# A third row buffer for the first stage's convolutions, in the room of the gates' small tiles

## The chip, the cores and the metric

The kernel runs on one core of one Trainium2 chip. The metric is the device time of one execution in microseconds (us). The core has engines that run side by side and wait for each other by semaphores: PE (TensorE: matmuls and transposes, with its weight loads, PEld), DVE (VectorE), ACT (ScalarE), POOL (GpSimd) and SP (SyncE, which here only issues DMAs). Each engine takes its instructions in the order in which the program gives them. SBUF is the working memory, 128 partitions; sizes below are in bytes of one partition.

## The reference

One layer of an encoder over 16 meta tokens and 1024 tokens of width 1024. What the change touches is in branch A, a gated DeltaNet with 8 heads:

```
h = rmsnorm(h_res, norm1_w[l])
proj = h @ w_in[l]
(q, k, v, z, b_raw, a_raw, sc_b, sc_c, sc_x, gate_a, gate_b) = jnp.split(proj, SPLIT_POINTS, axis=-1)
o_dn = gated_deltanet_bidir(q, k, v, z, b_raw, a_raw, ...)
y_b = (sc_b * depthwise_conv_centred(sc_c * sc_x, sc_conv_w[l])) @ w_branch_sc[l]
...
# in gated_deltanet_bidir
qkv = jax.nn.silu(depthwise_conv_centred(jnp.concatenate([q, k, v], axis=-1), conv_w))
beta = jax.nn.sigmoid(b_raw)
g = -jnp.exp(A_log) * jax.nn.softplus(a_raw + dt_bias)
o_fwd = chunk_gated_delta_rule(qp, kp, vp, gp[:, :, 0], bp[:, :, 0])
o_bwd = flip(chunk_gated_delta_rule(flip(qp), flip(kp), flip(vp), flip(gp[:, :, 1]), flip(bp[:, :, 1])))
```

Each of q, k and v goes through a centred convolution of five taps and SiLU; branch B has a convolution of three taps (the "short" one). beta and g, the gates, are small: 16 columns of b and 16 of a for each token. The scan of a head goes over chunks, forward and backward at once. What follows (merge, output projection, SwiGLU, last norm) is in later stages that the change leaves alone.

## The kernel before, in words

Every matmul in fp32 accuracy is made of three passes over operands split into a high and a low part, so PE does most of the work. The first stage (to about 1000 us) computes the input projection column block by column block, and the DeltaNet scans between.

**Units of dense work.** A unit is one block of 128 columns of `w_in`. `pick` (L922) gives out the next: K, Q, V of each head (`u_qkv`, L366; the order is in `qkv_units`, L906), then fill units: z (`u_z`), the short convolution's C, X and B (`u_short`, L416), and gates (`u_gate`). Which kind comes is set by how far the scans have got (`qkv_ok`). The matmuls of a unit are at L331.

**Rows.** A K, Q or V unit writes its result, 1040 columns wide in three chunks, twice by ACT: plain into a *row* (L387), and times the middle tap into `kq` or `vT` (L388). The row is a tile `ra` of 1044 floats, 4,176 bytes, from `row_buffer` (L339); POOL clears its edges (L385, L386). A short unit C also takes a row (its edge is cleared at L424), and X multiplies into the same row (L428, L431).

**Jobs.** The convolution of a row is vector work that is spread over time. `conv_job` (L347) makes it in two halves; in each, four operations at L354 add the outer taps, ACT takes the tanh (L359) and one operation at L362 finishes SiLU. The `yield` behind each tells the time at which the next step may be written. `short_job` (L401) is the same for the short convolution (L405, L410), `fs_job` (L483) is the elimination of a head's triangular systems: 62 small vector operations in turn (L490, L494).

**The planner.** The order of all instructions in this stage is written out when the program is made. Four clocks `T` estimate where each engine is. After each three matmuls, `run_streams` (L966) advances the heads' streams that are due: `g_decay`, `g_norm` (L530), `g_inv` (L622, which starts `fs_job`) and `g_scan` (L744); then `pump` (L302) writes out steps of jobs until DVE's clock is 700 ns past PE's. Jobs stand in lanes (conv, short, fs, norm); of the lanes that are ready the one with the least weighted time spent is served (`WEIGHT`, L267: 1.0 for conv and short, 0.33 for fs). Only the first job of a lane runs.

**Forcing.** A new row needs a free buffer. `row_buffer` therefore calls `force` (L258) on the job of the last row but one: it writes out all that is left of that job, and of jobs before it in its lane, at once, whatever the steps' ready times. The list `raws` holds the jobs in the order of their rows.

**Streams of a head.** `g_norm` starts when the K and Q jobs of its head are done. It turns k and q (copies from L560 on), makes norms (cc, L592), and later products of k and q (L582, with L612 and L616 on DVE). `g_inv` sends blocks through DRAM, starts the elimination, sends back, and finishes with small matmuls (L705 to L736). `g_scan` turns v into `vS` (L763), and for each step makes r on DVE (L805), which PE needs at L813; its output leaves at L898. A product loop starts when the decay factors of its head are there, and those wait for the scan before the last.

**The gates.** `g_gates` (L1200) runs once, early in the stage, between dense work: ACT and DVE make beta and the decays in tiles BA, a_, e_, z_, z2, sr and two gc, from the pool c1, 4,608 bytes together; PE reads gc at L1267 and L1279. They are not used again. `vS`, the scans' turned values, is a single buffer of 9 x 128 floats, 4,608 bytes, in the pool dn.

Of the kernel before, what the change touches and what calls it, by code (L numbers as in the profile page):

```python
# [8 lines left out]
F32 = mybir.dt.float32  # L9
# [7 lines left out]
P = 128  # L17
# [20 lines left out]
def encoder_layer(ctx: ExitStack, tc: tile.TileContext, x, meta, norm1_w, w_in,  # L38
# [16 lines left out]
    def uid(s):  # L55
        cnt["n"] += 1
        return f"{s}_{cnt['n']}"
# [144 lines left out]
    c1 = ph1.enter_context(tc.tile_pool(name="c1", bufs=1))  # L202
    d1 = ph1.enter_context(tc.tile_pool(name="d1", bufs=1))
# [14 lines left out]
    def on(e, ns, ready=0.0):  # L218

        T[e] = max(T[e], ready, T["pe"]) + ns  # L220
        return T[e] + TOPE
# [8 lines left out]
    def A(n):  # L230
        return on("act", 144 + 0.834 * n)
# [26 lines left out]
    def force(job):  # L258

        for q in lanes.values():  # L260
            if job in q:
                while not job.done:
                    while not q[0].done:
                        q[0].step()
                    q.pop(0)
# [71 lines left out]
    raws = []  # L337

    def row_buffer():  # L339
        if len(raws) >= 2:  # L340
            force(raws[-2])
        return d1.tile([P, 1044], F32, tag="ra", name=uid("ra"), bufs=2)

    def half_buffer():
        return d1.tile([P, 520], F32, tag="rb", name=uid("rb"), bufs=3)
# [20 lines left out]
    def u_qkv(h, i, w):  # L366
# [12 lines left out]
        for ci, (t0, n) in enumerate(QUERY if i == 1 else QCH):  # L379
            po = psm()  # L380
            yield from dense_steps(po, w, hx, t0, n, sweep=(h == i == ci == 0))
            if raw is None:
                raw = row_buffer()
                if i != 1:
                    nc.gpsimd.memset(raw[:, 0:2], 0.0)  # L385
                nc.gpsimd.memset(raw[:, L + 2:L + 4], 0.0)  # L386
            nc.scalar.copy(raw[:, 2 + t0:2 + t0 + n], po[:, :n])  # L387
            nc.scalar.activation(dst[:, t0:t0 + n], po[:, :n], AF.Copy, scale=wc[:, 2, col:col + 1])  # L388
            A(n)
            A(n)  # L390
            sub["rows"] = 2 + t0 + n if ci < 2 else L + 4
            if ci == 1:
                job = enqueue("conv", conv_job(raw, dst, col, sub, META if i == 1 else 0))
                raws.append(job)
# [21 lines left out]
    def u_short(j, i, w):  # L416
        st_ = shorts[j]
        if i < 2:
            for t0, n in ((14, 322), (336, 320), (656, 384)):
                po = psm()  # L420
                yield from dense_steps(po, w, hx, t0, n)
                if "cx" not in st_:
                    st_["cx"] = row_buffer()
                    nc.gpsimd.memset(st_["cx"][:, 1026:1028], 0.0)  # L424
                    raws.append(Job(iter(())))
                sl = st_["cx"][:, t0 - 14:t0 - 14 + n]
                if i == 0:
                    nc.scalar.copy(sl, po[:, :n])  # L428
                    A(n)
                else:  # L430
                    nc.vector.tensor_tensor(out=sl, in0=po[:, :n], in1=sl, op=ALU.mult)  # L431
                    V(n)
            if i == 1:
                st_["yc"] = []
                st_["job"] = enqueue("short", short_job(st_["cx"], j, st_["yc"]))
                raws[st_["ri"]] = st_["job"]
            else:
                st_["ri"] = len(raws) - 1
        else:
            for i2 in range(2):  # L440
                po = psm()
                yield from dense_steps(po, w, hx, META + 512 * i2, 512)
                force(st_["job"])
                yc = st_["yc"][i2][:, :512]
                nc.vector.tensor_tensor(out=yc, in0=po, in1=yc, op=ALU.mult)
                V(512)
                nc.sync.dma_start(p_d[j][:, 512 * i2:512 * i2 + 512], yc)
# [752 lines left out]
    def g_gates():  # L1200

        small_v = lambda: on("dve", 240)
        BA = c1.tile([P, 9, 32], F32, name="BA")
        dtb, alg = (c1.tile([P, 16], F32, name=n) for n in ("dtb", "alg"))
        nc.sync.dma_start(dtb, dt_bias.rearrange("a b c -> a (b c)").broadcast_to([P, 16]))
        nc.sync.dma_start(alg, A_log.rearrange("a b c -> a (b c)").broadcast_to([P, 16]))
        nc.gpsimd.memset(BA, 0.0)
        gcs = [c1.tile([P, 8, 9], F32, name=f"gc{d}") for d in range(2)]
        for gc in gcs:
            nc.gpsimd.memset(gc, 0.0)  # L1210
        pba = psd()
# [1 line left out]
        for c in range(9):  # L1213
            t0, p = (META + c * P, P) if c < 8 else (0, META)
# [3 lines left out]
        pv = pba.rearrange("p (c a n) -> p c a n", c=8, a=2)  # L1218
        nc.scalar.copy(BA[:, 0:8], pv[:, :, 0])
        nc.scalar.copy(BA[:META, 8], pbm[:META, 0:32])  # L1220
        A(512)
        yield T["act"] + HOP
        nc.vector.tensor_tensor(out=BA[:, 0:8], in0=pv[:, :, 1], in1=BA[:, 0:8], op=ALU.add)
        nc.vector.tensor_tensor(out=BA[:META, 8], in0=pbm[:META, 32:64], in1=BA[:META, 8], op=ALU.add)
        a_ = c1.tile([P, 9, 16], F32, name="a_")
        nc.vector.tensor_tensor(out=a_, in0=BA[:, :, 16:32], in1=dtb.unsqueeze(1).broadcast_to([P, 9, 16]), op=ALU.add)
        e_ = c1.tile([P, 9, 16], F32, name="e_")
        nc.vector.tensor_scalar(out=e_, in0=a_, scalar1=-1.0, scalar2=None, op0=ALU.mult)
        nc.vector.tensor_tensor(out=e_, in0=e_, in1=a_, op=ALU.min)
        yield on("dve", 1400)  # L1230
# [2 lines left out]
        nc.scalar.activation(beta, BA[:, :, 0:16], AF.Tanh, scale=0.5)  # L1233
        A(400)
        yield T["act"] + HOP
        z_ = c1.tile([P, 9, 16], F32, name="z_")
        nc.vector.tensor_scalar(out=z_, in0=e_, scalar1=2.0, scalar2=None, op0=ALU.add)
        nc.vector.reciprocal(z_, z_)
        nc.vector.tensor_tensor(out=z_, in0=z_, in1=e_, op=ALU.mult)
        z2 = c1.tile([P, 9, 16], F32, name="z2")  # L1240
        nc.vector.tensor_tensor(out=z2, in0=z_, in1=z_, op=ALU.mult)
        on("dve", 900)
        yield T["dve"]
        sr = c1.tile([P, 9, 16], F32, name="sr")
        nc.vector.tensor_scalar(out=sr, in0=z2, scalar1=2.0 / 17, scalar2=2.0 / 15, op0=ALU.mult, op1=ALU.add)
        small_v()
        for k in (13, 11, 9, 7, 5, 3, 1):
# [51 lines left out]
    dn = ph1.enter_context(tc.tile_pool(name="dn", bufs=1))  # L1299
    meta_inv = [dn.tile([P, P], F32, name=f"meta_inv{i}") for i in range(2)]  # L1300
    for m_ in meta_inv:
        nc.gpsimd.memset(m_, 0.0)
    SPL = (4, 6, 8, 10)
    decs.append([g_gates(), T["pe"], None])
    while done < H or qkv_units or fill_units or any(ahead):
        u = ahead.pop(0)
# [595 lines left out]
```

## Time and profile before

| | |
|---|---|
| median of three runs | 1979.19 us (1978.93 to 1982.11) |
| the profiled execution | 1981.91 us |
| its span, first to last instruction | 1980.1 us |
| mean granted clock of PE | 0.996 |
| busy: PE, DVE, ACT, POOL | 98%, 74%, 44%, 8% |
| row tiles: copies at L387, at L428 | 72, 24 |
| operations at L354 for q and k, for v | 128, 64 |

The profile is of one execution; its page gives each engine's busy time, the chain of work that ended last, and groups of instructions by line. A row of a group says which engine and line, what is written and read (`out<-in`), shapes, count, and busy time. In a timeline a row has its start and length in us, and in brackets how long the engine stood idle before it and what ended that. "issue" is a wait that the profile ascribes to nothing. In a view of waits a row has the engine that waited and its line, then what it waited for, the sum in us, the number of times and the longest.

### The profile page before, as it was taken

Reading aid. Unit: us, or ns where it says so; the run is one execution under the profiler, and the core shown is the slowest. Engines: PE = TensorE matmul, PEld = TensorE weight load, DVE = VectorE, ACT = ScalarE, POOL = GpSimd, SP = SyncE. Lnnn points to the kernel's source line nnn. Section 1 sums busy time; section 2 is a strip of 40 time slices with the busy share of each in tenths; the row PEclk is TensorE's granted clock in tenths of the full one; section 3 lists DMA queues with packets and bytes.
Section 4 is the critical chain, followed back from the end, with each engine's and each line's share of the span. In section 5 each row is a group of like instructions: output and inputs, shape, how many; then the busy total and the mean of one; then the engine's idle time right before and its main releaser. Section 6 shows DMA issues by size and latency. Waiting matters only on the chain.

```text
span 1980.1 us, 31950 instructions
## 1 busy us (share of the span) xinstructions
PE 1949.2 (98%) x11944; PEld 1705.7 (86%) x11944; DVE 1471.3 (74%) x2801; ACT 868.0 (44%) x2013; POOL 159.2 (8%) x457
## 2 busy tenths in 40 slices
PE   8999999999999999999999999999999999999998
PEld 8998899999999999998888888887888888878886
DVE  4888587888888888786348798559888777756574
ACT  5365435555555555433435545234233232224343
POOL 4002011120212120100000000000000000000001
PEclk9999999999999999999999999999999999999999
DMA  4123322222222222224287523333675454576554
GB/s 144 46 87 101 91 85 72 81 65 83 63 75 71 72 73 75 71 73 157 91 299 249 206 90 121 115 111 133 234 244 181 139 175 147 191 271 231 192 185 145
DMA packets 243136, 264.11 MB, mean 133 GB/s; under 512 B 46820, under 2 KB 166933, under 8 KB 240549
## 3 DMA queue, kind: packets, MB, share of 16 engines
q1 hardware_dynamic: 242981, 262.07, 40.9%
q8 instruction: 94, 1.54, 0.3%
q14 instruction: 61, 0.50, 0.1%
HBM read 189.58 MB, written 72.44 MB: 132 GB/s over the span
## 4 chain that ended last, share of the span: by engine, by line
PE 89%; DVE 7%; ACT 2%; DMA 1%; issue 1%; SPq 0%; POOL 0%; POOLq 0%; DVEq 0%; ACTq 0%
PE pm L331 31%; PE pm L1383 5%; PE pd L1383 4%; PE pe L1383 3%; PE pm L1659 3%; PE pm L1657 3%; PE pm L1658 3%; PE pd L1657 2%; PE pd L1658 2%; PE pd L1659 2%; DVE kq L354 2%; PE pe L1659 2%; PE pe L1657 2%; PE pe L1658 2%; PE pd L813 2%; PE pd L830 1%
## 5 line engine op out<-in xcount | busy, mean ns | idle before, releaser
L331 PE MATMUL pm<-hTh,wh 128*128 128x320 f32 (+4 forms) x1328 | 486.6, 367 | 0.1
L331 PE MATMUL pm<-hTh,wl 128*128 128x320 f32 (+4 forms) x1328 | 451.0, 340 | 0.0
L331 PE MATMUL pm<-al,wh 128*128 128x320 f32 (+4 forms) x1328 | 450.4, 340 | 0.5 <-DVE al L1045 0.5
L331 PEld LDWEIGHTS pm<-hTh,wl 128*128 128x128 f32 x1328 | 249.5, 188 | 15.6
L331 PEld LDWEIGHTS pm<-hTh,wh 128*128 128x128 f32 x1328 | 250.5, 189 | 14.5 <-ACT kq L388 0.3
L331 PEld LDWEIGHTS pm<-al,wh 128*128 128x128 f32 x1328 | 250.9, 189 | 13.4 <-DVE al L1045 0.7
L87 DVE TENSOR_TENSOR al<-raw,ring_h 128x1024 fp32r<-128x1024 f32 x73 | 88.3, 1223 | 67.2 <-ACT ring_h L86 67.0
L86 ACT CAST ring_h<-raw 128x1024 fp32r<-128x1024 f32 x73 | 76.5, 1053 | 107.1 <-PE pd L1801 39.3
L939 DVE TENSOR_TENSOR wl<-raw,wh 128x512 fp32r<-128x512 f32 x122 | 83.7, 686 | 28.5 <-ACT wh L942 28.0
L354 DVE SCALAR_TENSOR_TENSOR kq<-ra,wc,kq 128x520 f32<-128x520 f32 (+1 forms) x128 | 96.3, 752 | 10.2 <-ACT kq L388 7.8
L128 POOL TENSOR_SCALAR ss<-ss 128x1 f32<-128x1 f32 x13 | 4.7, 361 | 961.6 <-ACT b L1811 609.5
L494 DVE TENSOR_TENSOR fP<-fP,tm 128x135 f32<-128x135 f32 (+23 forms) x248 | 72.2, 291 | 7.4
L490 DVE TENSOR_TENSOR tm<-fP,fN 128x135 f32<-128x135 f32 (+23 forms) x248 | 72.7, 293 | 6.4
L942 ACT CAST wh<-raw 128x512 fp32r<-128x512 f32 x122 | 75.1, 617 | 1.4 <-PE pm L331 1.3
L820 ACT ACTIVATE w<-pd,small 128x128 f32<-128x128 f32 x128 | 40.1, 365 | 78.0 <-PE pd L813 69.8
L842 DVE SCALAR_TENSOR_TENSOR S<-S,eGl,pd 128x128 f32<-128x128 f32 x104 | 31.9, 345 | 54.8 <-PE pd L830 30.2
L87 DVE TENSOR_TENSOR raw<-pair,raw 128x1024 fp32r<-128x1024 f32 (+1 forms) x42 | 48.2, 1148 | 30.2 <-ACT raw L86 29.9
L86 ACT CAST raw<-pair 128x1024 fp32r<-128x1024 f32 (+1 forms) x42 | 41.7, 993 | 57.6 <-PE pd L1383 27.5
L87 DVE TENSOR_TENSOR wl<-pair,wh 128x1024 fp32r<-128x1024 f32 (+1 forms) x42 | 48.2, 1148 | 22.1 <-ACT wh L86 22.0
L86 ACT CAST wh<-pair 128x1024 fp32r<-128x1024 f32 (+1 forms) x42 | 41.7, 992 | 46.5 <-PE pd L1383 24.9
L1338 DVE TENSOR_TENSOR b<-pd,b 128x512 f32<-128x512 f32 x59 | 39.7, 688 | 28.7 <-PE pd L1659 28.6
L1338 DVE TENSOR_TENSOR b<-pm,b 128x512 f32<-128x512 f32 x58 | 39.1, 686 | 21.6 <-PE pm L1659 19.4
(653 smaller groups left out, 4934.9 us busy)
## 6 DMA issues: line engine op xcount, KB each, us to landing
raw<-in_w_in_dram SPq DMA_DIRECT2D x64, 512.0 KB
raw<-in_w_gate_up_dram SPq DMA_DIRECT2D x44, 512.0 KB
sums<-in_w_down_dram SPq DMA_DIRECT2D x22, 512.0 KB
t_d<-sums SPq DMA_DIRECT2D x11, 1024.0 KB
raw<-s_d SPq DMA_DIRECT2D x44, 256.0 KB
raw<-t_d SPq DMA_DIRECT2D x44, 256.0 KB
act_d<-b SPq DMA_DIRECT2D x43, 256.0 KB
raw<-act_d SPq DMA_DIRECT2D x33, 256.0 KB
```

The lines of the kernel that those rows point to most:

```text
L86: nc.scalar.copy(hi, src)
L87: nc.vector.tensor_tensor(out=lo, in0=src, in1=hi.bitcast(F32), op=ALU.subtract)
L331: mm(po[:, :n], (wl if j == 2 else wh)[:, k], xl[k][:, t0:t0 + n] if j == 1 else xh[k][:, t0:t0 + n], start=(i == 0), stop=(i == 3 * KT - 1))
L354: nc.vector.scalar_tensor_tensor(out=acc, in0=raw[:, h0 + t:h0 + t + hn], scalar=wc[:, t, col:col + 1], in1=acc, op0=ALU.mult, op1=ALU.add)
L490: nc.vector.tensor_tensor(out=tv, in0=fP[:, 0:r, j:j + 1].broadcast_to([P, r, n]), in1=fN[:, j:j + 1, j + 1:32].broadcast_to([P, r, n]), o ...
L939: nc.vector.tensor_tensor(out=u[1][1][:, k], in0=u[2][:, k], in1=u[1][0][:, k].bitcast(F32), op=ALU.subtract)
L942: nc.scalar.copy(u[1][0][:, k], u[2][:, k])
L1338: add = lambda out, a, b: nc.vector.tensor_tensor(out=out, in0=a, in1=b, op=ALU.add)
L1383: mm(bank[t], a[:, c], b, start=fresh, stop=first and k == 3 and j == 2, skip_group_check=not first)
L1657: mm(po, ah[:, k], bhk, start=k == 0, stop=False)
L1658: mm(po, ah[:, k], blk, start=False, stop=False)
L1659: mm(po, al[:, k], bhk, start=False, stop=k == 3)
```

## The change

`row_buffer` gets three buffers in place of two, and forces the job of the last row but two. To make room, the gates' tiles become slices of one buffer of vS's tag, so their 4,608 bytes in c1 are free; the third row takes 4,176. The instructions of the gates are the same ones, with the same shapes.

```diff
     def row_buffer():
-        if len(raws) >= 2:
-            force(raws[-2])
-        return d1.tile([P, 1044], F32, tag="ra", name=uid("ra"), bufs=2)
+        if len(raws) >= 3:
+            force(raws[-3])
+        return d1.tile([P, 1044], F32, tag="ra", name=uid("ra"), bufs=3)
...
     def g_gates():
...
-        BA = c1.tile([P, 9, 32], F32, name="BA")
+        scratch = dn.tile([P, 9, P], F32, tag="vS", name=uid("scratch")).rearrange("p a b -> p (a b)")
+        BA = scratch[:, 0:288].rearrange("p (c n) -> p c n", c=9)
+        a_, e_, z_, z2, sr = (scratch[:, 288 + 144 * i:432 + 144 * i].rearrange("p (c n) -> p c n", c=9) for i in range(5))
...
-        gcs = [c1.tile([P, 8, 9], F32, name=f"gc{d}") for d in range(2)]
+        gcs = [scratch[:, 1008 + 72 * d:1080 + 72 * d].rearrange("p (h c) -> p h c", h=8) for d in range(2)]
...
-        a_ = c1.tile([P, 9, 16], F32, name="a_")
...
-        e_ = c1.tile([P, 9, 16], F32, name="e_")
...
-        z_ = c1.tile([P, 9, 16], F32, name="z_")
...
-        z2 = c1.tile([P, 9, 16], F32, name="z2")
...
-        sr = c1.tile([P, 9, 16], F32, name="sr")
```

## The prediction

> **What bounds the kernel now.** I begin with the head of the page, then cut the span into stretches (the view of busy time by windows; its columns are the stretch, its length, and the busy time of PE, weight loads, DVE, ACT and POOL, then the granted clock).
>
> ```profile
> span 1980.1 us, 31950 instructions
> PE 1949.2 (98%) x11944; PEld 1705.7 (86%) x11944; DVE 1471.3 (74%) x2801; ACT 868.0 (44%) x2013; POOL 159.2 (8%) x457
> ```
> ```profile
> 46.00:360.00 314.00, 311.87 (x2249) 285.02 (x2248) 240.71 (x602) 155.30 (x475) 41.49 (x142) 1.00 0.27 78
> 360.00:780.00 420.00, 412.64 (x3501) 392.10 (x3500) 356.45 (x939) 232.72 (x769) 63.89 (x190) 1.00 0.26 72
> 780.00:1000.00 220.00, 218.12 (x1634) 193.13 (x1633) 139.18 (x330) 85.20 (x252) 18.07 (x46) 0.99 0.32 99
> 1000.00:1980.00 980.00, 966.28 (x4290) 797.90 (x4288) 712.19 (x895) 369.25 (x466) 15.68 (x33) 0.99 0.54 184
> ```
>
> PE is the bound everywhere: 98% of the span. The edited code works in the first stage, which ends near 1000 us. From 46 to 1000 us PE is idle for 2.1 + 7.4 + 1.9 = 11.4 us of 954. The change adds no matmul and takes none away, so these 11.4 us (and one dip of the clock, below) are all it can win. What they are, the view of PE's waits over that stretch says:
>
> ```profile
> PE pd L813 <- DVE r L805: 6.1, 5, 1.6
> PE pd L713 <- issue: 1.9, 1, 1.9
> PE pe L582 <- DVE PQ L616: 1.3, 4, 0.5
> PE pe L1267 <- DVE gc L1259: 1.2, 1, 1.2
> PE pe L83 <- DVE Nm L565: 0.5, 1, 0.5
> PE pe L1267 <- ACT eGl L1275: 0.3, 1, 0.3
> ```
>
> The largest is five waits, 6.1 us, of the scan's matmul at L813 for the vector operation of L805. The timeline around the first of them shows why DVE is late (DVE first, then POOL, then PE):
>
> ```profile
> 361.18 2.30 DVE L354 SCALAR_TENSOR_TENSOR kq<-ra,wc,kq 128x504 f32<-128x504 f32 x3
> 364.17 0.68 DVE L362 SCALAR_TENSOR_TENSOR kq<-rb,kq 128x504 f32<-128x504 f32 x1 [0.69 <-ACT rb L359]
> 364.77 3.21 DVE L354 SCALAR_TENSOR_TENSOR kq<-ra,wc,kq 128x520 f32<-128x520 f32 x4
> 368.69 0.70 DVE L362 SCALAR_TENSOR_TENSOR kq<-rb,kq 128x520 f32<-128x520 f32 x1 [0.70 <-ACT rb L359]
> 369.30 0.60 DVE L805 SCALAR_TENSOR_TENSOR r<-pd,negEG,vS 128x128 f32<-128x128 f32 x2
> ...
> 368.10 0.10 POOL L424 MEMSET ra<- 128x2 f32 x1 [26.07 <-DVE kq L354]
> ...
> 369.96 0.71 PE L813 MATMUL pd<-r,NP 128*128 128x128 f32 x4 [1.56 <-DVE r L805]
> ```
>
> Nine vector operations of one convolution, Q's (the 504-wide first half marks it), stand in a block of 8.2 us, 361.18 to 369.39, and the scan's L805 is queued behind them. That block is `force`: the short convolution's row (its memset is L424) wants the older of two buffers, so everything left of Q's job is written out at once. Inside it DVE waits twice, 0.69 + 0.70 = 1.4 us, for ACT's tanh; outside a block the planner fills such time. `conv_job` yields the tanh's end, but `force` ignores what a job yields, so the planner's clock for DVE runs early by about that. PE's 1.56 us fit. Five waits of POOL's L424 for this line, 122.2 us in all (idle time that costs nothing), say that it happens five times, as do the five waits of PE:
>
> ```profile
> POOL ra L424 <- DVE kq L354: 122.2, 5, 27.2
> ```
>
> **The change part by part.** *The tiles.* The gates' BA, a_, e_, z_, z2, sr and gc become slices of one vS buffer. Every instruction stays, on its engine and with its shape: nothing. Two waits could be new. The scratch lies in the pool opened after the loading stage; its memsets follow meta_inv's, which wait already. And the first scan's vS must wait for the gates' last reader:
>
> ```profile
> POOL meta_inv L1302 <- PE pe L1051: 9.9, 1, 9.9
> ...
> L1279 PE MATMUL pe<-U2b,gc x2: 270/270/271, 95.0 to 95.1; 128*72 128x128 f32 x2
> ...
> L763 ACT ACTIVATE vS<-pd,small x72: 359/368/437, 151.6 to 882.3; 128x128 f32<-128x128 f32 x72
> ```
>
> It is done at 95, vS is first written at 151.6: 56 us of cover. If it went, the first scan alone would start later, with dense work to fill the time.
>
> *The third row.* Rows come in the order K, Q, V, short. With two, the short row forces Q and the next K forces V; with three, the short row forces K, the next K forces Q, the next Q forces V. Jobs of the lane run in order, and Q had begun before its block, so K is done by then. So the block should go and Q run as the pump finds room. **First term: −6.1 us** (ends 0 and −6.1; I take all, since the wait's whole cause is shown five times).
>
> The start has blocks too, as nine rows follow each other and DVE is nearly full; the gates' chain is planned among them. The 1.2 + 0.3 + 0.5 = 2.0 us of PE at L1267 and L83 (for L1259, L1275, L565) belong to the gates and the first head, behind this:
>
> ```profile
> 76.47 0.70 DVE L362 SCALAR_TENSOR_TENSOR kq<-rb,kq 128x520 f32<-128x520 f32 x1 [0.77 <-ACT rb L359]
> ...
> 83.67 0.51 DVE L1259 TENSOR_TENSOR gc<-sr,alg 128x64 f32<-128x64 f32 x4
> ```
>
> DVE hardly rests between, so the lost 0.77 us may still be missing at 83.67. But with DVE this full a third row is soon used up and some forcing remains. Ends 0 and −2.0; I take half, **−1.0**. Of the four waits on L616 (1.3 us) some follow the tail of V's job, forced by the next K:
>
> ```profile
> 608.43 0.70 DVE L362 SCALAR_TENSOR_TENSOR vT<-rb,vT 128x520 f32<-128x520 f32 x1 [0.76 <-ACT rb L359]
> ...
> 610.45 0.42 DVE L616 TENSOR_TENSOR PQ<-pe,PQ 128x256 f32<-128x256 f32 x1
> ```
>
> V is now wanted one row later. Ends 0 and −1.3; I take a third, **−0.4**.
>
> *What is late next.* The vector work is only put in another order, with DVE 356.45 / 420 = 85% busy. A new order has late operations of its own: at best none, at worst five as long as today's (+6.1). The nearest row for unforced lateness is the same four waits at L616: **+1.3**. The memset of a row and ACT's copies (L387, L428) only wait less.
>
> *The chain of heads.* Q's block sits inside the elimination of the head before (`fs_job`, whose last steps are at L490 and L494) and stretches it by 8.2 us; but it also ends Q early, which lets the next head's `g_norm` start:
>
> ```profile
> 369.70 0.28 ACT L560 COPY kn<-pe 128x128 f32<-128x128 f32 x1
> ...
> 382.78 0.18 DVE L490 TENSOR_TENSOR tm<-fP,fN 128x16 f32<-128x16 f32 x1
> ...
> 383.34 0.76 DVE L354 SCALAR_TENSOR_TENSOR vT<-ra,wc,vT 128x520 f32<-128x520 f32 x1
> ...
> 391.43 0.69 DVE L362 SCALAR_TENSOR_TENSOR vT<-rb,vT 128x520 f32<-128x520 f32 x1
> ...
> 385.53 0.20 DVE L592 TENSOR_TENSOR small<-beta,small 128x18 f32<-128x18 f32 x1
> ...
> L582 PEld LDWEIGHTS pe<-kq x16: 186/188/191, 398.1 to 415.6; 128*128 128x128 f32 x16
> ```
>
> Unforced, Q waits for the elimination (lane weights 0.33 against 1.0 favour it; V is left until 383 today). That ends near 383 − 8 = 375. V, which the pump runs right after the elimination today, takes about 9 us for its first half (383.34 to 392.12); the block has left two halves less one operation of Q. With lighter company than V has (the short job comes later) I estimate 13 us, so Q ends at about 388 instead of 369.4: 19 us later. Today `g_norm` has cc (L592) 16 us after Q and then idles 12.6 us until its products start (398.1). So the next head's products start 19 − 12.6 = 6 us later, and its own elimination is 8 us shorter: about even. Meanwhile dense work fills PE, and there is some left when the last scan ends (chain of waits):
>
> ```profile
> 972.59 0.44 PE pd L833 x4
> ...
> 982.81 15.01 PE pm L331 x66
> ```
>
> That is 997.8 − 973.0 = 25 us in which a later chain costs nothing; an earlier one gains nothing either. Term 0.
>
> *Instruction supply.* One wait, 1.9 us at L713, is released by nothing that the profile names. It lies in a burst of tiny matmuls, while the instruction queue brings a block, and the clock is at half speed right after it (0.51 over 3.5 us costs 3.5 × 0.49 = 1.7 us):
>
> ```profile
> q8 instruction: 1, 0.02, 2.4%
> ...
> 901.95 0.21 PE L713 MATMUL pd<-NP,T 32*32 32x32 f32 x1 [1.88 <-issue]
> ...
> 902.95:906.45 3.50, 3.50 (x10) 2.69 (x9) 2.31 (x4) 1.93 (x5) 0.00 (x0) 0.51 0.16 57
> ```
>
> Eight heads have two bursts each, and one of sixteen is hit; another order may miss it or hit two. Price 1.9 + 1.7 = 3.6 us each way; I take 0.
> The Trainium skill, "Runtime: NRT & Kernel Launch", § Instruction fetch mechanics, says that sequential fetch in 16 KiB blocks is mostly hidden; by that the order couldn't matter here and this price would be nothing, which row 901.95 speaks against. The Trainium skill, "TensorE: Matmul & The Clock Gate", Part 1, has the clock halve only after an idle window of about 3.4 us; by that the five waits of at most 1.6 us cost no clock, as the trace agrees (1.00 from 360 to 780 us), but neither would the 1.9 us, where it does not.
>
> **The sum.** −6.1 − 1.0 − 0.4 + 1.3 = **−6.2 us**. The profiled execution took 1981.9 us (its span 1980.1), so 1975.7 for it; it lies 2.7 us above the median of three, 1979.19, within their spread. On the median: **1973.0 us**. About 0.2%, 4 us, is what a measurement of this kernel can tell from no change.
>
> **The rivals.**
> *A. The late work only moves.* The wait returns at the next forced row: the next K forces Q's end, or DVE at 85% is late elsewhere. For it: V's end is forced today just there (608.43). Against: Q comes before V in the lane, and it is V's end that falls there today. Taking +6 for new waits in place of +1.3 leaves −1.5: 1977.7. Chance 0.18.
> *B. Block gone, one more hit of the instruction supply.* −6.2 + 3.6 = −2.6: 1976.6. Chance 0.11. (One fewer would be 1969.4, inside the forecast.)
> *C. Slower: the chain of heads becomes the bound.* Place: Q unforced, starved by the elimination, holds back `g_norm`. Over five heads it must lose more than 25 / 5 = 5 us a head before PE idles behind the last scan; the estimate above is −2 (6 later, 8 shorter), so Q would have to end some 7 us later still, 26 us after today's. At 8 us a head: 5 × 8 − 25 = 15, less 6.2: +9, 1988. For it: today's early start of `g_norm` is the block's own gift, and the slack of 12.6 us is less than the 19 needed. Against: shorter eliminations, and a product loop that needn't wait for the decays. Chance 0.10, and 0.03 more for A with one or two hits of the supply (+2 to +6).
> *D. It doesn't do what it says:* forcing still binds at the short row. That needs K unfinished there, while today Q has begun before it. Its time is 1979; 0.02, counted with no change.
>
> **Chances and range.** The forecast has 0.56, its own range 1968.5 to 1975.2. Faster by over 0.2% (under 1975.2): 0.56. Within: A, B and D, 0.31. Slower (over 1983.2): 0.13. Lowest by the bounds: −6.1 − 2.0 − 1.3 − 3.6 = −13, 1966. Leaving out that corner and most of C, the range is 1967.5 to 1983.0.
>
> **What would show it.** Right: no block of nine L354/L362 before L805, the waits of L813 on L805 near nothing, POOL's L424 released long before, Q's convolution after the elimination, cc later, and PE still without a gap up to 1000 us. Wrong: waits of PE on DVE of the same sum at other lines (A); a second "issue" wait with a clock of 0.5 (B); empty PE during the last scan or less than 66 matmuls behind it (C); the blocks still there (D).

## The result and the profile after

| | before | after |
|---|---|---|
| median | 1979.06 us (1977.75 to 1982.61, 6 runs) | 1972.19 us (1970.73 to 1977.01, 6 runs) |
| the profiled execution | 1981.91 us | 1972.62 us |
| its span | 1980.1 us | 1970.9 us |
| its mean granted clock | 0.996 | 0.999 |

The ratio is 0.9964, 95% interval 0.9953 to 0.9975: faster by 0.36%; the medians lie 6.9 us apart. The forecast was 1973.0 with a range of 1967.5 to 1983.0. The time came out as forecast; several of the terms behind it did not, and the experiments are mostly about those. Three executions of the kernels below, at 2145 to 3242 us, ran at a lower clock (0.56 to 0.85), and the medians and ratios leave them out.

First the head of the page of after, and its first stage in the view by windows (columns as in the prediction):

```profile
span 1970.9 us, 31897 instructions
PE 1944.7 (99%) x11944; PEld 1701.4 (86%) x11944; DVE 1469.3 (75%) x2801; ACT 869.8 (44%) x2013; POOL 159.5 (8%) x457
```
```profile
46.00:1000.00 954.00, 947.77 (x7413) 874.36 (x7412) 734.30 (x1869) 475.68 (x1496) 124.24 (x378) 1.00 0.29 81
```

Counts of PE, DVE, ACT and POOL are those of before, so it is the same work in another order. PE's idle time from 46 to 1000 us is 954.0 − 947.8 = 6.2 us where it was 11.4. What is left of it, by the view of PE's waits over that stretch of after:

```profile
PE pd L813 <- DVE r L805: 2.9, 5, 1.0
PE pd L83 <- ACT NP L892: 1.5, 1, 1.5
PE pd L781 <- DVE w L779: 0.5, 1, 0.5
PE pd L713 <- issue: 0.4, 1, 0.4
PE pm L331 <- issue: 0.4, 1, 0.4
PE pd L795 <- DVE S L842: 0.3, 1, 0.3
```

The reader should not take the first row for what is left of the old five waits. Those are gone; these are five others. The timeline shows one of the two that are near 1 us (ACT first, then DVE, then PE); the other, at 453.31, stands behind the same two lines, and the remaining three are of 0.3 us:

```profile
350.29 0.62 ACT L942 CAST wh<-raw 128x512 fp32r<-128x512 f32 x1
...
350.93 0.69 DVE L939 TENSOR_TENSOR wl<-raw,wh 128x512 fp32r<-128x512 f32 x1 [1.60 <-ACT wh L942]
351.54 0.60 DVE L805 SCALAR_TENSOR_TENSOR r<-pd,negEG,vS 128x128 f32<-128x128 f32 x2
...
352.20 0.71 PE L813 MATMUL pd<-r,NP 128*128 128x128 f32 x4 [0.98 <-DVE r L805]
```

L939 splits weights and stands ahead of L805 on DVE; it waits 1.60 us for a cast on ACT. No step of a convolution stands in this row of waits. And where the block of nine stood before, DVE now finishes the elimination, and Q's convolution follows in loose pieces with other work between:

```profile
367.06 0.19 DVE L494 TENSOR_TENSOR fP<-fP,tm 128x16 f32<-128x16 f32 x1
367.16 0.73 DVE L354 SCALAR_TENSOR_TENSOR kq<-ra,wc,kq 128x504 f32<-128x504 f32 x1
367.81 0.74 DVE L898 SCALAR_TENSOR_TENSOR NP<-pd,cols,vS 128x512 f32<-128x512 f32 x1
...
385.54 0.70 DVE L362 SCALAR_TENSOR_TENSOR kq<-rb,kq 128x520 f32<-128x520 f32 x1
```

POOL's memset of a short row waits for the convolution once in place of five times:

```profile
POOL ra L424 <- DVE kq L354: 6.6, 1, 6.6
```

Last, the chain of heads. Each scan opens with L779; its row in the view by lines gives the first and the last of eight, and that of L833 the end of the last scan (before's is in the prediction, 973.0). For before:

```profile
L779 DVE TENSOR_SCALAR w<-pd,small x8: 342/350/351, 230.7 to 915.8; 128x128 f32<-128x128 f32 x8
```

For after:

```profile
L779 DVE TENSOR_SCALAR w<-pd,small x8: 342/350/352, 215.6 to 929.4; 128x128 f32<-128x128 f32 x8
L833 PE MATMUL pd<-v,PQ x256: 270/275/275, 223.6 to 986.4; 128*128 128x128 f32 x128
```

The first scan starts 15.1 us earlier, and yet the last one starts 13.6 us later (and ends at 986.7, 13.7 later): a head takes (929.4 − 215.6) / 7 = 102.0 us where it took (915.8 − 230.7) / 7 = 97.9. The loss lies in the last five heads, those whose Q was forced in before: their scans follow each other by (929.4 − 400.7) / 5 = 105.7 us in after and by (915.8 − 418.1) / 5 = 99.5 in before (the third scan's L779 starts at 400.67 and at 418.07).

### The profile page after: what moved, and what is told of

It reads as the page before. It is cut to its first block, busy times and chain, and to the rows that moved or that the text cites. A ratio compares the mean times of both kernels' runs of the same rounds, so it can differ in the third digit from the quotient of the medians.

```text
span 1970.9 us, 31897 instructions
## 1 busy us (share of the span) xinstructions
PE 1944.7 (99%) x11944; PEld 1701.4 (86%) x11944; DVE 1469.3 (75%) x2801; ACT 869.8 (44%) x2013; POOL 159.5 (8%) x457
## 4 chain that ended last, share of the span: by engine, by line
PE 92%; DVE 3%; ACT 2%; DMA 1%; issue 1%; SPq 0%; POOL 0%; POOLq 0%; DVEq 0%; ACTq 0%
PE pm L331 34%; PE pm L1380 5%; PE pd L1380 4%; PE pe L1380 3%; PE pm L1656 3%; PE pm L1654 3%; PE pm L1655 3%; PE pd L1656 2%; PE pd L1654 2%; PE pd L1655 2%; PE pe L1656 2%; PE pe L1654 2%; PE pe L1655 2%; PE pd L813 2%; PE pe L582 1%; PE pm L1797 1%
## 5 line engine op out<-in xcount | busy, mean ns | idle before, releaser
L331 PE MATMUL pm<-hTh,wh 128*128 128x320 f32 (+4 forms) x1328 | 484.7, 366 | 0.4 <-issue 0.4
L331 PE MATMUL pm<-hTh,wl 128*128 128x320 f32 (+4 forms) x1328 | 450.6, 340 | 0.0
L331 PE MATMUL pm<-al,wh 128*128 128x320 f32 (+4 forms) x1328 | 449.7, 340 | 0.5 <-DVE al L1045 0.5
L331 PEld LDWEIGHTS pm<-hTh,wl 128*128 128x128 f32 x1328 | 249.2, 188 | 15.6
L331 PEld LDWEIGHTS pm<-al,wh 128*128 128x128 f32 x1328 | 250.4, 189 | 13.5 <-DVE al L1045 0.7
L331 PEld LDWEIGHTS pm<-hTh,wh 128*128 128x128 f32 x1328 | 250.2, 189 | 13.5 <-ACT hTh L1039 0.2
L939 DVE TENSOR_TENSOR wl<-raw,wh 128x512 fp32r<-128x512 f32 x122 | 84.0, 689 | 45.7 <-ACT wh L942 42.9
L490 DVE TENSOR_TENSOR tm<-fP,fN 128x135 f32<-128x135 f32 (+23 forms) x248 | 72.3, 292 | 9.0 <-POOL tm L660 2.8
L494 DVE TENSOR_TENSOR fP<-fP,tm 128x135 f32<-128x135 f32 (+23 forms) x248 | 71.8, 289 | 7.4
L130 POOL TENSOR_TENSOR small<-small,minus_half 128x9 f32<-128x9 f32 x16 | 29.9, 1870 | 405.3 <-DVE small L877 251.0
```

What stands on the lines that cost most here:

```text
L331: mm(po[:, :n], (wl if j == 2 else wh)[:, k], xl[k][:, t0:t0 + n] if j == 1 else xh[k][:, t0:t0 + n], start=(i == 0), stop=(i == 3 * KT - 1))
L490: nc.vector.tensor_tensor(out=tv, in0=fP[:, 0:r, j:j + 1].broadcast_to([P, r, n]), in1=fN[:, j:j + 1, j + 1:32].broadcast_to([P, r, n]), o ...
L494: nc.vector.tensor_tensor(out=fP[:, 0:r, j + 1:32], in0=fP[:, 0:r, j + 1:32], in1=tv, op=ALU.subtract)
L939: nc.vector.tensor_tensor(out=u[1][1][:, k], in0=u[2][:, k], in1=u[1][0][:, k].bitcast(F32), op=ALU.subtract)
```

## The experiments

Each edit is against the kernel named. Ratios are against the kernel before, run beside each (its median was 1978.6 to 1980.4 us there), with their 95% intervals.

**The tiles alone.** Against after: two rows and the old order, so that only the gates' tiles have moved.

```diff
-        if len(raws) >= 3:
-            force(raws[-3])
-        return d1.tile([P, 1044], F32, tag="ra", name=uid("ra"), bufs=3)
+        if len(raws) >= 2:
+            force(raws[-2])
+        return d1.tile([P, 1044], F32, tag="ra", name=uid("ra"), bufs=2)
```

> The gates' tiles are moved into the buffer of vS as in the change, but there are two row buffers and the job of the last row but one is forced, as before. My theory (the gain is from the order of the vector work, which the third row permits): same time as before, 1979 us, within 4; the five waits of L813 on L805 are still there, 6.1 us in all, and the block of nine operations stands before them. Rival (moving the tiles itself brings something, say an earlier start of the gates): 1972 to 1975 us.

Measured 1978.28 us, ratio 0.9986 (0.9977 to 0.9996). All that PE waited for before is there again: L813 6.2 us in five, L713 1.7, and the 1.5 us at the gates' matmul (L1264 here, L1267 in before, with "issue" as the cause this time). Moving the tiles brings 0.14%, and by the interval 0.23% at most.

**The room without the new order.** Against after: three buffers, but the last row but one is still forced.

```diff
-        if len(raws) >= 3:
-            force(raws[-3])
+        if len(raws) >= 2:
+            force(raws[-2])
```

> Three row buffers, but the job of the last row but one is forced as before, so every instruction stands where it stood; only POOL's memsets and ACT's copies of a row may start earlier. My theory: 1979 us, within 4, and the five waits of L813 still about 6 us. Rival (the room itself counts: rows no longer wait for the old convolution): the gain of the change, 1972 us, with PE's waits near those of the changed kernel.

Measured 1978.21 us, ratio 0.9991 (0.9983 to 1.0). POOL's wait of the short row's memset is gone, since there is a free row, but PE's waits are not. The first row of this kernel's view of them:

```profile
PE pd L813 <- DVE r L805: 6.2, 5, 1.6
```

So room and tiles together are worth 0.1% here, by the interval 0.2% at most. What the buffer buys is that the program may write its instructions in another order, and nearly all of the 0.36% comes with that order.

**The short rows in the old way.** Against after: a short row forces the last row but one; K, Q and V rows the last but two.

```diff
-    def row_buffer():
-        if len(raws) >= 3:
-            force(raws[-3])
+    def row_buffer(back=3):
+        if len(raws) >= back:
+            force(raws[-back])
...
-                    st_["cx"] = row_buffer()
+                    st_["cx"] = row_buffer(2)
```

> The changed kernel, but the row of a short unit forces the last job but one (Q) as before; all other rows force the last but two. My theory: the block of Q is back inside the elimination, with some 6 us of waits at L813, and the heads' g_norm starts early again; the last scan ends well before the dense work, 15 us or more. Time between the two, 1977 us or more, unless the start of the stage brings more than the 1 to 2 us that I gave it. Rival (the start and the other rows bring the gain): 1973 us or less.

Measured 1987.81 us, ratio 1.0035 (1.0022 to 1.0047): slower than before, which no theory had foreseen. The two largest of its waits of PE, and one block (DVE, then ACT, then PE):

```profile
PE pm L331 <- ACT ra L428: 5.8, 3, 2.6
PE pd L813 <- DVE r L805: 3.7, 7, 1.3
```
```profile
466.62 3.08 DVE L354 SCALAR_TENSOR_TENSOR kq<-ra,wc,kq 128x504 f32<-128x504 f32 x4
...
474.24 0.64 ACT L359 ACTIVATE rb<-kq 128x520 f32<-128x520 f32 x1 [3.88 <-DVE kq L354]
474.78 0.41 ACT L428 COPY ra<-pm 128x322 f32<-128x322 f32 x1
...
475.25 0.64 PE L331 MATMUL pm<-hTh,wh 128*128 128x322 f32 x1 [2.56 <-ACT ra L428]
```

With K and V forced later, Q has not begun when the short row comes, and the block is all of Q, from 466.62 on. Now ACT is held up too: the copy of the short row stands behind Q's second tanh, and the dense matmuls need the bank that this copy empties. A forced block can cost more than the vector operation queued behind it. This accounts for part of the loss only: the stage has 14.2 us of idle PE in place of 11.4, and its clock was at half twice for 3.4 us (0.51 from 475.2 us, 0.50 from 683.4) in place of once, some 4.5 us together, while the median is 7.4 us above that of before beside it. The first scan starts at 215.3 us as in after, so the early start comes from the rows of K, Q and V.

**Only the short rows in the new way.** The reverse, with three buffers.

```diff
-    def row_buffer():
-        if len(raws) >= 3:
-            force(raws[-3])
+    def row_buffer(back=2):
+        if len(raws) >= back:
+            force(raws[-back])
...
-                    st_["cx"] = row_buffer()
+                    st_["cx"] = row_buffer(3)
```

> Three row buffers; only the row of a short unit forces the last job but two, all other rows the last but one. My theory: the five waits of L813 go, about 6 us; the start of the stage is as before (waits at L1267 and L565 of about 2 us stay); heads follow each other more slowly than before, as in the changed kernel. Time 1973 to 1975 us. Rival (start and other rows bring the gain): 1978 us or more. If the slower heads matter more than I think, PE idles behind the last scan, and the time is 1976 or more with the waits at L813 gone.

Measured 1984.88 us, ratio 1.0019 (1.0011 to 1.0028). This is the prediction's rival C, seen. PE waits of L813 are down to two, and a scan starts every (940.2 − 230.4) / 7 = 101.4 us, as in after, but without the early start:

```profile
L779 DVE TENSOR_SCALAR w<-pd,small x8: 346/351/352, 230.4 to 940.2; 128x128 f32<-128x128 f32 x8
```
```profile
PE pm L1380 <- ACT raw L86: 7.2, 1, 7.2
...
PE pd L813 <- DVE r L805: 1.2, 2, 0.9
```

The 7.2 us at L1380 are the entry of the next stage. What holds it is on SP's queue. A row of its timeline is start, length, line, what is moved and how many; L901 stores a scan's output, L1344 (L1347 in before) loads the next stage's weights. In before, in after and in this kernel, in this order:

```profile
983.63 0.37 SPq L901 DMA_DIRECT2D o_d<-NP  x1
1000.72 2.25 SPq L1347 DMA_DIRECT2D pair<-in_w_in_dram  x4
```
```profile
993.26 1.55 SPq L901 DMA_DIRECT2D o_d<-NP  x2
996.92 2.23 SPq L1344 DMA_DIRECT2D pair<-in_w_in_dram  x4
```
```profile
1001.75 1.75 SPq L901 DMA_DIRECT2D o_d<-NP  x2
1005.60 2.33 SPq L1344 DMA_DIRECT2D pair<-in_w_in_dram  x4
```

In before the load goes out 17 us after the last output; in the other two 3.7 and 3.9 us after it. There the last scan sets when the next stage starts. In this kernel the granted clock was 0.50 for 10.2 us from inside that gap on. PE was busy for 5.31 us of them, so this costs another 5.31 × 0.50 = 2.7 us:

```profile
1006.50:1016.70 10.20, 5.31 (x13) 4.10 (x14) 5.29 (x7) 2.33 (x5) 0.00 (x0) 0.50 1.02 361
```

**The instruction stream moved.** The kernel before with fewer warming matmuls at its start, so that all that follows stands 64 PE instructions earlier in the stream (in exchange the clock comes up to full later, at 12 us in place of 5).

```diff
-        keep_warm(44)
+        keep_warm(12)
```

> The kernel before with 32 fewer of the idle transposes at its very start (12 in place of 44), so that all later PE instructions lie 64 places earlier in the instruction stream; nothing else is changed. My theory (the wait of L713 that nothing releases, and the half clock behind it, come from where a block of instructions ends): the wait of 1.9 us near 900 us goes or turns up in another burst of small matmuls; if it goes, the time is 2 to 4 us less than before, 1975 to 1977 us; PE's waits for DVE (L813 6.1 us) stay. Rival (it hangs on the data or on the DMAs of that moment): the wait stays at L713 near 900 us with its 1.9 us, time 1979.

Measured 1977.27 us, ratio 0.999 (0.9981 to 0.9999). The wait at L713 and the half clock behind it are gone; the five waits of L813 stay at 6.1 us. From the view by windows, before and then this kernel:

```profile
895.00:910.00 15.00, 13.12 (x229) 10.11 (x227) 10.59 (x13) 4.16 (x9) 0.00 (x0) 0.89 0.45 154
```
```profile
895.00:910.00 15.00, 15.00 (x272) 11.78 (x271) 13.36 (x16) 4.64 (x10) 0.00 (x0) 1.00 0.54 191
```

In the traces of the four kernels with the old stream (before, the tiles alone, the room without the new order, and before with one more late gate unit, below) the stall of 1.4 to 1.9 us and the half clock were there at 902 to 904 us each time; in this one and in after they were not. So they hang on where the stream stands, or on the moment at which it gets there, which the edit moves too. That after is rid of them by the shift that its new order makes, and not by anything that the third row is for, is the likely reading; it was not tried by itself.

**A truer clock for forced steps.** In `force`, each step first sets the planner's clock to the time at which the step is ready, which the prediction had named as the fault behind the 1.56 us. Once on before and once on after.

```diff
                     while not q[0].done:
+                        T["dve"] = max(T["dve"], q[0].ready)
                         q[0].step()
```

> The kernel before, two rows and the same jobs forced, but force puts the planner's clock of DVE to each step's ready time before it writes the step, so the block has its true length in the plan. My theory (PE waits at L813 since the planner's clock runs early by the tanh waits in the block): the blocks stay, but the five waits of L813 shrink from 6.1 us to under 2, with other dense work put before L813; the gates' chain is not faster than before (first copy at L560 at 108 us or later), so the start does not gain. Time 1973 to 1977 us. Rival (the block is late for L805 however it is planned): waits of 6 us stay, 1979.

> The changed kernel with the same correction of force. By the runs so far hardly a block is left in it behind the start, so little can be won: waits of L813 on L805 stay near 3 us, and the time is that of the changed kernel, 1972 us, within 3. If the chain of heads gets slower by even a few us, PE idles behind the last scan, as there is no dense work left over there: then 1975 or more.

On before: 2047.87 us, ratio 1.0345 (1.0331 to 1.0359), against an expectation of a gain. The waits of the scan's matmul for r did fall, from 6.1 to 2.8 us, but the last scan starts at 1013.0 us in place of 915.8, and PE runs dry. From this kernel's view of PE's waits (lines here and in the next are one higher) and its view by windows, with the clock at 0.71:

```profile
PE pd L706 <- DVE XT L691: 13.2, 1, 13.2
...
PE pd L814 <- DVE r L806: 2.8, 5, 0.8
```
```profile
980.00:1090.00 110.00, 62.79 (x480) 51.67 (x480) 63.50 (x119) 34.63 (x104) 2.42 (x3) 0.71 0.36 129
```

On after: 1980.13 us, ratio 1.0005 (0.9995 to 1.0015), its last scan 7.9 us later (937.3 in place of 929.4) and with this row, in its view of PE's waits, where after has 1.5 us:

```profile
PE pm L1381 <- ACT raw L86: 7.9, 1, 7.9
```

Two things follow. A planner's estimate that is wrong isn't made better by a more honest number at one place; that everything else was timed by it is the likely reason. And in after hardly any cover is left. The chain's last output goes out 4.0 us later than in after (997.24 in place of 993.26), and the next stage's first matmul comes 4.2 us later (1006.90 in place of 1002.68) and then runs at half clock until 1012.0, which costs 2.5 us more. That fits the profiled executions, 6.4 us apart; the medians are 7.9 apart.

**The weight of the convolution.** After, with the convolution's weight as low as the elimination's.

```diff
-    WEIGHT = {"conv": 1.0, "short": 1.0, "fs": 0.33, "norm": 0.1}
+    WEIGHT = {"conv": 0.33, "short": 1.0, "fs": 0.33, "norm": 0.1}
```

> The changed kernel with the conv lane's weight at 0.33, as the elimination's, so that Q's convolution and the elimination take turns. My theory (in the changed kernel a head's g_norm starts late because Q waits for the elimination): g_norm's first copy (L560) comes earlier by 10 us or more in heads 3 to 7, the last scan ends earlier, and dense work is left behind it; the wait of 1.5 us at the last scan's output goes. Time 1968 to 1972 us. Rival (a longer elimination loses as much as an earlier Q gains): the last scan ends at the same time within 5 us, and the time is 1972 or more.

Measured 1973.11 us, ratio 0.9969 (0.9959 to 0.9979). The instructions of every engine came out in the same order as after's, so it is a repetition of after and says nothing of the weight but that it doesn't decide. The reason, as read from `enqueue`: a lane that becomes busy starts at the least time spent of *all* lanes, and with a weight of 0.1 that is norm's. So conv, whose sum has grown for long, stands behind a fresh fs.

**More late gates.** `LATE` sets how many gate units are kept back; of 9 one, of 10 two run at the end of this stage, right behind the other dense units (48 matmuls each, at L119 to L121). On before and on after.

```diff
-LATE = 9
+LATE = 10
```

> The kernel before with one more gate unit (48 dense matmuls, 11 us) left for behind the stage, so that much less dense work stands beside the scans. My theory (25 us of dense work behind the last scan were cover that cost and gained nothing): the last scan ends where it did, near 973 us, with about 57 dense matmuls behind it in place of 105; the time is 1979 us, within 4. Rival (the cover is not there to spare): 1984 or more.

> The changed kernel with the same one gate unit less beside the scans. My theory (the changed kernel has used up that cover: 3 dense matmuls are left behind its last scan): PE idles in the last scans, 5 to 11 us in all, perhaps with a half clock, and the time is 1977 to 1986 us. Rival (the later gate units fill in just as well, and the slower heads cost nothing): 1972 us, within 3.

Measured 1978.97 us, ratio 1.0 (0.9991 to 1.0008), and 1971.81 us, ratio 0.9965 (0.9953 to 0.9977). Neither moves, but neither takes cover away as the expectations had it, since these left out the matmuls at L119 to L121. On before, 105 + 48 dense matmuls stand behind the last scan, and here 57 + 96, the same 153. On after it is 3 + 48; here, 30 of the 96 stand among the last scan's steps and 66 behind it. The 1.5 us at the entry of the next stage are gone, and the time is that of after. What less cover costs is therefore not shown by these two.

**The starved lane.** After, with one line changed so that a lane that becomes busy starts level with the busiest of the other waiting lanes:

```diff
         if not lanes[lane]:
-            spent[lane] = max(spent[lane], min(spent.values()))
+            spent[lane] = max([spent[lane]] + [spent[k] for k, q in lanes.items() if q and k != "norm"])
```

> The changed kernel; a lane that becomes busy starts at the largest time spent of the busy lanes (norm apart) instead of the least of all, so the weights decide between elimination and convolution (3 to 1) and Q no longer waits for the elimination's end. My theory (g_norm starts late because Q is starved): the first copy at L560 comes 5 us or more earlier in heads 3 to 7, the last scan ends earlier than 986 us and leaves dense work behind it; the 1.5 us wait at the last scan's output goes; 1969 to 1973 us. Rival (a stretched elimination loses as much as the early norm gains, or more): the last scan ends as late or later, and PE idles behind it: 1973 to 1985 us.

Measured **1965.83 us**, ratio 0.9942 (0.993 to 0.9954), faster than both kernels: the interval just meets that of after (0.9953 to 0.9975), and the medians lie 6.4 us apart (6.0 from the late-gates form of after, run beside it). Its view of PE's waits has this row alone, and the first stage holds 1.55 us of idle time in 954:

```profile
PE pd L813 <- DVE r L805: 1.3, 3, 1.0
```
```profile
46.00:1000.00 954.00, 952.45 (x7440) 879.59 (x7438) 739.02 (x1877) 477.12 (x1501) 124.78 (x378) 1.00 0.30 85
```
```profile
L779 DVE TENSOR_SCALAR w<-pd,small x8: 343/350/352, 221.5 to 903.0; 128x128 f32<-128x128 f32 x8
```

A head takes (903.0 − 221.5) / 7 = 97.4 us, as in before, and the last five take 99.1 each (the third scan starts at 407.42). `g_norm`'s first copy comes 10 to 20 us earlier than in after in heads 3 to 7 (the last one at 776.0 in place of 796.1). The edit touches nothing but the lanes, so it was the lanes that made after's chain slow. Q's wait shows in heads 3 and 4, where the copy comes 9.1 and 2.5 us behind the end of the elimination of the head before, in place of 23.5 and 23.1. In heads 5 to 7 it comes 5 to 7 us behind it, no nearer than in after, and it is the elimination that ends earlier; that this is inherited from heads 3 and 4 was not tried apart.

**The same line without the third row.** The edit of the last experiment, on before.

> The kernel before (two row buffers, gates' tiles in their own pool) with the one changed line of e11: a lane that becomes busy starts with the weighted time of the busiest of the other waiting lanes, so that the convolution isn't kept behind the elimination. Question: is the third row still worth anything once the lanes share fairly? My theory: the blocks are made by the forced order, not by the lanes, so with two rows the short row and the next K still force them and the waits of L813 on L805 (6.1 us before) stay at 4 to 6 us; the chain of heads runs near 100 us a head. Then 1973 to 1978, so that the third row is worth 7 to 12 us beside the fair line. Rival 1, the fair line is all of the gain and the third row none: 1965 to 1968, with the waits of L813 at 1 to 2 us. Rival 2, the line acts against the forced order (Q waits for the elimination and is forced later anyhow): 1980 or more, with longer waits at L813.

Measured 1987.57 us, ratio 1.0039 (1.0024 to 1.0053): slower than before. None of the three theories fits as a whole: the waits of L813 are as small as the first rival had them, the time is the second rival's. From its view of PE's waits:

```profile
PE pe L582 <- DVE PQ L616: 5.5, 6, 3.1
PE pe L83 <- ACT jk L544: 4.1, 4, 1.2
...
PE pd L813 <- DVE r L805: 0.8, 4, 0.2
```
```profile
412.56 0.70 DVE L362 SCALAR_TENSOR_TENSOR vT<-rb,vT 128x520 f32<-128x520 f32 x1 [0.76 <-ACT rb L359]
413.84 0.69 DVE L939 TENSOR_TENSOR wl<-raw,wh 128x512 fp32r<-128x512 f32 x1 [0.58 <-ACT wh L942]
414.45 0.42 DVE L616 TENSOR_TENSOR PQ<-pe,PQ 128x256 f32<-128x256 f32 x1
```

The longest wait lies behind V's end, with DVE waiting for ACT's tanh inside it, as in the old block of Q. The late work has moved to V and to the norms, which is what rival A had in mind. PE is idle for 15.2 us of the stage in place of 11.4, and its clock was at 0.50 from 414.3 to 421.1 us, with the 3.1 us wait, beside the dip near 913. That V's end is forced there by the next K, and why L544 is late, was read from the code and not tried apart. What the run settles is that the line needs the third row: alone it costs 0.4%; the third row as in after gains 0.4%; both together gain 0.6%.

## Why the prediction was right, point by point

The total was right, within a microsecond on the median. By its terms, in the profiled first stage:

| term | predicted | measured |
|---|---|---|
| five waits of L813 behind Q's block | −6.1 | −6.1 |
| start and gates (L1267, and L83 on L565) | −1.0 | −2.0 |
| waits on L616 | −0.4 | −1.3 |
| new late waits (L813, L781, L795) | +1.3 | 2.9 + 0.5 + 0.3 = +3.7 |
| chain of heads (L83 at the last scan's output, entry of the next stage) | 0 | 1.5 + 1.5 = +3.0 |
| instruction supply in this stage | 0 | −1.9 − 1.7 + 0.4 + 0.4 = −2.8 |
| sum | −6.2 | −5.5 |

The measured sum answers to the first matmul of the next stage, which came 5.9 us earlier. Its row before, and after:

```profile
1008.54 0.39 PE L1383 MATMUL pm<-hTh,raw 128*128 128x512 f32 x1
```
```profile
1002.68 0.47 PE L1380 MATMUL pm<-hTh,raw 128*128 128x512 f32 x1 [1.52 <-issue]
```

The two profiled executions lie further apart, 9.3 us. Of the rest some 2.7 us are one place in the last stages, near 1772 us of before, where its PE waited for weights for 1.8 us in place of 0.8 and the clock then was at half for 3.4 us; the work there is the same, and half clocks outside the first stage came and went between the traces, so this is not counted for the change. The medians are 6.9 apart.

**What held.** *The first term.* The block was the short row's `force`, and it is gone; the room alone leaves it (1978.21), the order removes it. *Q's own times*, in part by luck. Q was forecast to end near 388 and ended at 386.2 (385.54 + 0.70); but the elimination was over at 367.25 and not near 375, and Q then took 19 us and not 13. The two errors cancel. *The tiles* cost nothing (1978.28). *D* is refuted.

**Mis-sized: new late waits.** The prediction took +1.3, by the row of four waits at L616, and had +6 as rival A. They are 3.7, in the middle between the two. The two largest, 1.0 us each, are not at a convolution but behind a weight split that waits for ACT; the small ones were not followed up. The step's own bound, +6.1, was as near as the row it chose.

**The step that failed: the chain of heads.** "About even", −2 us a head, is 102.0 − 97.9 = +4.1 us a head, and +6.2 over the last five. The estimate was the next head's products (the matmuls of L582) 6 us later, and its own elimination (L490 and L494) 8 us shorter. From the timelines of both kernels, in us:

| head, counted from 0 | 3 | 4 | 5 | 6 | 7 |
|---|---|---|---|---|---|
| products start, before | 398.3 | 499.0 | 597.7 | 697.4 | 798.7 |
| products start, after | 406.9 | 517.5 | 612.4 | 715.3 | 813.5 |
| later by | 8.6 | 18.5 | 14.7 | 17.9 | 14.8 |
| elimination, before | 44.7 | 45.4 | 42.4 | 44.6 | 46.5 |
| elimination, after | 33.5 | 30.5 | 42.2 | 39.6 | 42.0 |
| shorter by | 11.2 | 14.9 | 0.2 | 5.0 | 4.5 |

The elimination's gain is 7.2 us in the mean, about as forecast; the lateness is 14.9 in place of 6. For head 3, the one that the prediction followed, the step is nearly right: 8.6 later, 11.2 shorter. What it left out is the round that follows: a head that is late starts its own elimination later, and behind that the next head is kept again. In before, `g_norm`'s first copy (L560) in heads 3 to 7 comes 12 to 17 us ahead of the end of the elimination of the head before; in after it comes 1 to 24 us behind it, in every one of the five. Over seven intervals that makes 13.6 + 15.1 = 28.7 us. Two things hid it. The first scan starts 15.1 us earlier; the prediction had counted the start's blocks as waits of PE and not as a gain of the chain. And the cover, 25 us by the prediction's count of the dense work at L331, took what was left, from both ends: the chain's end moved back by 13.6 us, and the dense work's end forward, from 997.8 to about 987, where the last of it now starts at 986.4:

```profile
L331 PE MATMUL pm<-hTh,wh x1328: 302/337/586, 16.1 to 986.4; 128*128 128x512 f32 x52, 128*128 128x320 f32 x45, 128*128 128x384 f32 x44, 128*128 128x322 f32 x29
```

About 24 of 25 us are spent, and 3.0 us of waits show at the end. They show although 48 more dense matmuls, of the late gate unit at L119 to L121, follow (from 987.2 us in after, from 997.7 in before), which the prediction did not count. The first 1.5 us are at the turning of the scan's output (L83, at 991.13), which is written among them and waits for ACT; the other 1.5 us come after the last of them, at the entry of the next stage, whose load goes out right behind the scan's last output. After stands at the point from which rival C decides. The two kernels that put the last scan's start another 7.9 and 10.8 us later (937.3 and 940.2 against 929.4) came out at 1980.13 and 1984.88. C was more likely than the 0.10 that it was given, and its threshold, a loss of over 5 us a head in five heads, was passed with 6.2; the early start made up for it.

**Mis-sized: instruction supply.** Taken as 0, with 3.6 either way, it paid 2.8; by the shifted stream this is a matter of where the stream stands, and probably not of the third row.

So the errors cancelled: +2.4 for new waits and +3.0 for the chain against −1.9 for the two small terms and −2.8 for the supply, together +0.7. The forecast stands on its largest term; that the rest summed to so little was luck.

**The signs that the prediction named.** No block before L805, POOL's memset early, Q behind the elimination: as written. The waits of L813 on L805, which were to be near nothing, are 2.9 us. For A, waits of the same sum at other lines: 3.7 of 6.1. For C, fewer than 66 dense matmuls behind the last scan: three are left at L331, and yet PE waits for 3.0 us only. The sign was there, its price not yet.

## What to carry to other kernels

Another buffer in a kernel whose order is written out ahead is worth what the order makes of it: test it once with the old order and once with the new. When a forced block goes, ask who ended early thanks to it, and let the delay run through all rounds of the loop, not one; then see how much of the cover behind the last round is left. A gain that uses up the cover is one change away from a loss, and here the next step was not more cover but the lane that kept Q waiting.

## What the runs showed of the hardware

In five traces a stall of 1.4 to 1.9 us that nothing in the trace releases, among 32x32 matmuls near 902 or 912 us, was followed by 3.4 us of clock at half (0.51 from 902.95 us in before), while the five waits of up to 1.6 us at L813 in before were not (granted clock 1.00 from 360 to 780 us). In the last experiment the clock was 0.51 from 912.6 to 916.0 us, behind this row:

```profile
911.99 0.18 PE L713 MATMUL pd<-NP,T 32*32 32x32 f32 x1 [1.61 <-issue]
```

Neither the length of the gap nor the size of the matmuls decides it. Among 128x512 matmuls of a late stage, a gap of 1.83 us in before (ended at 1772.02) was followed by half speed, and one of 1.62 us at the same place in the kernel with the room alone was not. And in the kernel with short rows in the old way, two gaps of nearly the same length stand at the same line, L331 waiting for L428. Here are the first, the clock behind it, and the clock behind the second (2.56 us, shown above at 475.25):

```profile
374.33 0.42 PE L331 MATMUL pm<-hTh,wh 128*128 128x322 f32 x1 [2.48 <-ACT ra L428]
...
374.30:377.70 3.40, 3.37 (x25) 3.37 (x26) 2.21 (x7) 3.40 (x13) 0.00 (x0) 1.00 0.24 58
475.20:478.60 3.40, 3.35 (x14) 3.31 (x15) 2.15 (x6) 1.49 (x4) 1.72 (x1) 0.51 0.26 55
```

What decides stays open. Where a stall falls depends on all that stands ahead of it in the stream, so a kernel can gain or lose 3.6 us by an edit that has nothing to do with the place.
